# Modulation columns on VectorE alone, in another order, in a three-block transformer kernel

## The chip, the core and the metric

The kernel runs on one core of a Trainium2 chip. TensorE multiplies matrices into PSUM banks, VectorE and ScalarE work on SBUF and PSUM, GpSimd on SBUF; SyncE's queue issues the loads of weights, GpSimd's queue the gathers. The metric is the time of one execution in microseconds (us) as the device measures it; lower is better.

## The reference, cut to what matters

Two transformer blocks over 256 image tokens (x) and, in the first, 256 context tokens (ctx), then a third block of another kind. Width 1024, all float32.

```
def _modulation(cvec, w_mod, b_mod):
    m = jax.nn.silu(cvec) @ w_mod + b_mod
    return jnp.split(m[:, None, :], 6, axis=-1)
...
    for l in range(DEPTH):
        m_x = _modulation(c, w_mod[l], b_mod[l])
        m_c = _modulation(c_ctx[None, :], w_mod[l], b_mod[l])
        h = _modulate(x, norm1_g[l], m_x[0], m_x[1])
        hc = _modulate(ctx, norm1_g[l], m_c[0], m_c[1])
        if last:
            kv_c = _ctx_keys_values(hc, lp)
        else:
            mix_c, kv_c = _token_mix(hc, lp, None, None)
        mix_x, _ = _token_mix(h, lp, ang, kv_c)
        x = x + m_x[2] * mix_x
        h2 = _modulate(x, norm2_g[l], m_x[3], m_x[4])
        x = x + m_x[5] * _peer(h2, w_pq[l], peer_keys[l], peer_down[l], peer_up[l])
        if not last:
            ctx = ctx + m_c[2] * mix_c
            hc2 = _modulate(ctx, norm2_g[l], m_c[3], m_c[4])
            ctx = ctx + m_c[5] * _peer(hc2, ...)
```

A modulation has 6 x 1024 numbers: 48 columns of 128 (one column on 128 partitions), each the product of 128 rows of a weight matrix (512 KB) with silu(c). Columns 0 to 15 (shift and scale of the first norm) are `FIRST`; the rest are needed from the end of the mix on. `_token_mix` is latent attention, a Fourier and a pooling branch under gates, and `_peer` selects 128 of 16384 experts for each token, whose rows (8 KB) are gathered from memory. The third block has the same modulation and experts, with windowed attention and an RWKV scan for its mix.

## The kernel before

Tokens are kept transposed (features on partitions), in two tiles of 128 tokens where the experts work. The code records operations; a list scheduler then puts each engine's in an order by priority (the length of what depends on an operation, plus a lift given to its stage), by planned positions of stages (`ORDER`) and by how many buffers of a name may be in use (`QUOTA`); all instructions then come from one line, L694. An engine carries out its own list strictly in order, SyncE its loads likewise.

The stages in order of time, with the profile's times of before: block 1 image mix (x0, 0 to about 459 us: set-up, modulations, projections, gates, attention), expert selection and gathers for the image (p0, p0g) with the context's mix (c0) beside them, experts of the context (q0, q0g, to 1960), the rest of block 2's image mix (x1, y1), its experts (p1, p1g, 2119 to 2790), the third block's mix (b2, to 3338), its experts (p2, p2g). An expert stage is 256 gathers, 128 for each tile, of 1 MB each by GpSimd's queue; VectorE makes the dot products with `h2tok` (the tile's tokens as rows) and part of the weighted sum into `accd`.

`mods(wt, cols, outs)` (L795) makes columns: it loads the 512 KB of a column into a `wm` buffer, and for each output either VectorE multiplies and accumulates in one instruction (`scalar_tensor_tensor` with `accum_out`), or GpSimd multiplies into `mp` and ScalarE sums up; then one add of the bias on 128x1. `emit` (L1803) calls it so: `FIRST` of block 1 for the image on VectorE and the context on GpSimd, before both h; columns 16 to 47 likewise (m0); then, with a lift of -1000, block 2's `FIRST` for both, its columns 16 to 47 for the image, and the third block's `FIRST`, all on VectorE (m1: 32 + 32 + 16 columns); and after the second expert stage the third block's columns 16 to 47 on GpSimd (n2). `load_c` makes silu(c) on all partitions (`cb`). `kvproj` projects keys and values; `mix` makes the gates and the sums of gated branches `x0y` (eight pairs of instructions on VectorE), `mix_attend` attention and the output. `gather` (L1234) clears `accd` for both tiles, and makes a tile's `h2tok` (eight transposes on TensorE, two copies on ScalarE) when its turn comes.

Of the kernel before, what the change touches and what calls it, by code (L numbers as in the profile page):

```python
# [15 lines left out]
BF16 = mybir.dt.bfloat16  # L16
AF = mybir.ActivationFunctionType
OP = mybir.AluOpType
# [678 lines left out]
class Kern:  # L697
# [70 lines left out]
    def setup(self):  # L768
# [12 lines left out]
        self.junk = [self.t([P, D], f"junk{i}", 1, BF16) for i in range(2)]  # L781
# [13 lines left out]
    def mods(self, wt, cols, outs, bufs=6):  # L795

        for j in cols:
            w = self.w(wt[j], "wm", bufs)
            for m, cb, b, eng in outs:
                o = m[:, j:j + 1]  # L800
                if eng is self.nc.vector:
                    eng.scalar_tensor_tensor(self.junk[0], w, 1.0, cb, op0=OP.mult, op1=OP.mult, accum_out=o)
                else:
                    q = self.t([P, D], "mp", 2)
                    eng.tensor_tensor(q, w, cb, op=OP.mult)
                    self.nc.scalar.activation(self.junk[1], q, AF.Copy, accum_out=o)
                eng.tensor_tensor(o, o, b[:, j:j + 1], op=OP.add)
# [5 lines left out]
    def mods2(self, m2, cols, eng):  # L813
        self.mods(self.A["wada"], cols, [(m2, self.cb2, self.col("ada_b"), eng)])
# [419 lines left out]
    def gather(self, sel, n, tab, xT, g2, erf):  # L1234
# [3 lines left out]
        accs = [self.t([P, D], f"accd{i}", bufs=1) for i in range(-(-n // P))]  # L1238
        for i, acc in enumerate(accs):
            self.ahead(i)  # L1240
            nc.gpsimd.memset(acc, 0.0)
        for i in range(NT):
            m = min(P, n - i * P)
            if m <= 0:
                break
            self.ahead(i)
# [6 lines left out]
            acc = accs[i][:m]  # L1253
# [549 lines left out]
def emit(K, out, stage=None):  # L1803
# [9 lines left out]
    if stage in ("mix2", "b2"):  # L1813
        K.begin("x0", {}, "x0")
        K.load_cb2()
        K.mods2(m2, FIRST + list(range(16, 48)), nc.vector)
        return block2(K, out, stage, m2)
# [33 lines left out]
    both = [(modx[0], cbs[0], bm[0], nc.vector), (modc[0], cbs[1], bm[0], nc.gpsimd)]  # L1851
    K.mods(A["wmod0"], FIRST, both)
    K.load_mix(0)
    h = norm1(xT, modx[0], 0)
    hc = K.ln(cT, K.gscale(modc[0], 8, n1[0], "gsc"), modc[0][:, 0:8], name="c")
    K.kvproj(0, hc, 0, False)
    K.kvproj(0, h, T, True)
# [4 lines left out]
    K.begin("m1", {}, "m1", None, -1000)  # L1862
    K.mods(A["wmod1"], FIRST, [(modx[1], cbs[0], bm[1], nc.vector), (modc[1], cbs[1], bm[1], nc.vector)])
    K.mods(A["wmod1"], range(16, 48), [(modx[1], cbs[0], bm[1], nc.vector)])
    K.load_cb2()
    K.mods2(m2, FIRST, nc.vector)

# [34 lines left out]
    K.begin("n2", {}, "n2", "q0g")  # L1902
    K.load_cb2()
    K.mods2(m2, range(16, 48), nc.gpsimd)
# [15 lines left out]
def block2(K, out, stage, m2):  # L1920
    nc, A, xT = K.nc, K.A, K.xT
    K.begin("b2", {"ps": 6, "pt": 2}, "b2", "p1s")
    h = K.ln(xT, K.gscale(m2, 8, K.col("norm1_g_2"), "gsc"), m2[:, 0:8], spans=TILES)
# [180 lines left out]
```

## Time and profile before

| | us |
|---|---|
| median of 3 runs | 4013.39 (4008.55 to 4016.52) |
| profiled execution | 4016.26 |
| span of its profile | 4014.3 |
| TensorE busy | 2998.6 |
| VectorE busy | 2881.5 |
| ScalarE busy | 2077.3 |
| GpSimd busy | 1703.4 |

The mean granted clock of TensorE is 0.874 of full speed. 1305 MB are moved, 1074 MB of them by the gathers. In these pages PE is TensorE, PEld its weight loads, DVE VectorE, ACT ScalarE, POOL GpSimd, SP SyncE; "sb" is SBUF, "bank" a PSUM bank. An idle time stands in square brackets with what ended it. A row "x8" joins eight instructions one behind the other. A stretch is read for the engine that is busy nearly all of it, and where none is, for the rate of the DMA.

### The profile page before, as it was taken

How to read it: one execution, taken by the hardware profiler on the slowest of the kernel's cores; microseconds unless marked ns; L12 is line 12 of the kernel's file. 1: busy time of each engine (PE TensorE's matmuls, PEld its weight loads, DVE VectorE, ACT ScalarE, POOL GpSimd, SP SyncE). 2: the span in 40 equal slices, each digit the busy share in tenths (PEclk: the TensorE clock that was granted, in tenths of full speed). 3: DMA queues.
4: the chain of work that ended last, by engine and by line, in shares of the span. 5: the costliest groups of instructions: out<-in, count | busy, mean ns of one | idle time of the engine just before them, and what ended most of it. 6: DMA issues, size and time to landing. Idle time of an engine off the chain costs nothing. (4 is left out here: it accounts for less than half of the span.)

```text
span 4014.3 us, 40650 instructions
## 1 busy us (share of the span) xinstructions
PE 2998.6 (75%) x10928; PEld 1776.5 (44%) x10928; DVE 2881.5 (72%) x6733; ACT 2077.3 (52%) x6342; POOL 1703.4 (42%) x1325
## 2 busy tenths in 40 slices
PE   5769863597796589976698856666899998766755
PEld 4556731365473246632275422222677776322221
DVE  6697799977889985566547997666444438986566
ACT  4222455655655676566755667766544324433322
POOL 5470134545434444345553454554111113465454
PEclk7879875799998899998899988877899989888888
DMA  5557798999999999999757999999210017999998
GB/s 211 207 201 246 267 371 357 407 390 419 381 416 420 374 415 418 413 421 421 311 200 321 384 421 421 415 421 392 79 56 9 30 40 307 413 417 421 422 421 354
DMA packets 219828, 1305.42 MB, mean 325 GB/s; under 512 B 24336, under 2 KB 28880, under 8 KB 88272
## 3 DMA queue, kind: packets, MB, share of 16 engines
q0 software_dynamic: 147456, 1073.81, 64.9%
q1 hardware_dynamic: 72144, 229.02, 15.9%
q8 instruction: 89, 1.46, 0.1%
q14 instruction: 139, 1.14, 0.1%
HBM read 1301.68 MB, written 1.05 MB: 325 GB/s over the span
## 5 line engine op out<-in xcount | busy, mean ns | idle before, releaser
L694 PE MATMUL bank<-sb 128*128 128x128 f32 (+6 forms) x10928 | 2998.6, 431 | 1009.3 <-ACT sb L694 894.9
L694 PEld LDWEIGHTS bank<-sb 128*128 128x128 f32 (+4 forms) x10928 | 1776.5, 197 | 2231.0 <-ACT sb L694 1342.6
L694 DVE SCALAR_TENSOR_TENSOR sb<-sb 128x1024 f32<-128x1024 f32 (+4 forms) x1794 | 2052.0, 1171 | 670.7 <-DMA sb<-in_tab_dram,sb 538.0
L694 ACT ACTIVATE sb<-sb 128x1 f32<-128x1 f32 (+3 forms) x5415 | 1682.3, 319 | 1315.5 <-DVE sb L694 1053.3
L694 POOL DMA_INDIRECT sb<-in_tab_dram,sb x1024 | 1344.8, 1313 | 1582.2 <-PE bank L694 781.5
L694 POOL TENSOR_TENSOR sb<-sb 128x256 f32<-128x256 f32 (+2 forms) x288 | 350.7, 1248 | 546.2 <-DVE sb L694 213.9
L694 ACT ACTIVATE sb<-bank 128x256 f32<-128x256 f32 (+6 forms) x458 | 182.3, 414 | 359.6 <-PE bank L694 331.1
L694 DVE TENSOR_TENSOR sb<-sb 128x32 f32<-128x32 f32 (+13 forms) x1035 | 309.4, 332 | 18.8 <-ACT sb L694 12.6
L694 ACT ACTIVATE sb<-bank,sb 128x256 f32<-128x256 f32 (+3 forms) x223 | 104.0, 474 | 245.8 <-PE bank L694 141.3
L694 DVE SCALAR_TENSOR_TENSOR sb<-bank,sb 128x128 f32<-128x128 f32 (+3 forms) x186 | 64.9, 380 | 121.5 <-ACT sb L694 77.5
L694 DVE TENSOR_TENSOR sb<-bank,sb 128x64 f32<-128x64 f32 (+5 forms) x180 | 72.6, 422 | 101.5 <-PE bank L694 97.8
L694 ACT ACT_TABLE_LOAD x102 | 130.9, 1283 | 5.6 <-DVE sb L694 1.6
L694 DVE TENSOR_TENSOR sb<-sb,bank 128x512 f32<-128x512 f32 (+1 forms) x96 | 56.7, 597 | 79.4 <-PE bank L694 76.3
L694 DVE FIND_INDEX8 sb<-sb 128x8 uint32<-128x128 f32 (+1 forms) x384 | 96.7, 260 | 0.0
L694 DVE DVE_READ_ACCUMULATOR sb<-sb 128x1 f32 x1152 | 94.8, 82 | 0.0
L694 DVE MAX8 sb<-sb 128x8 f32<-128x128 f32 (+1 forms) x384 | 84.7, 255 | 11.6 <-ACT sb L694 10.8
L694 DVE TENSOR_SCALAR sb<-sb 128x128 f32<-128x128 f32 (+6 forms) x232 | 57.0, 256 | 41.1 <-DMA sb<-in_cols_dram 16.9
L694 DVE TENSOR_REDUCE sb<-sb 128x16 f32<-128x800 f32 (+3 forms) x120 | 74.7, 634 | 0.1
L694 POOL MEMSET sb<- 128x1024 f32 x8 | 7.6, 955 | 156.9 <-PE bank L694 126.7
L694 DVE SCALAR_TENSOR_TENSOR sb<-sb,bank 128x256 f32<-128x256 f32 (+1 forms) x88 | 30.8, 368 | 44.2 <-PE bank L694 39.1
L694 DVE MATCH_VALUE_LOAD sb<-sb 128x8 f32 x576 | 46.6, 81 | 0.2 <-DVE sb L694 0.2
L694 DVE MATCH_REPLACE8 sb<-sb 128x128 f32<-128x128 f32 (+1 forms) x192 | 46.5, 250 | 0.0
(14 smaller groups left out, 112.3 us busy)
## 6 DMA issues: line engine op xcount, KB each, us to landing
sb<-in_win_dram SPq DMA_DIRECT2D x116, 512.0 KB
sb<-in_wmod_dram SPq DMA_DIRECT2D x96, 512.0 KB
sb<-in_wpq_dram SPq DMA_DIRECT2D x64, 512.0 KB
sb<-in_wada_dram SPq DMA_DIRECT2D x48, 512.0 KB
sb<-in_wout_dram SPq DMA_DIRECT2D x32, 512.0 KB
sb<-in_tab_dram,sb POOLq DMA_INDIRECT x1024
sb<-in_wo_dram SPq DMA_DIRECT2D x48, 256.0 KB
sb<-in_poolm_dram SPq DMA_DIRECT2D x6, 512.0 KB
```

The costliest lines, as they stand in the source:

```text
L694: getattr(getattr(nc, op.eng), op.meth)(*[res(x) for x in op.args], **{k: res(x) for k, x in op.kw.items()})
```

## The change

All columns are made by VectorE, and the bias is added once for eight columns. The image's `FIRST` columns of block 1 stand by themselves, then the image's `kvproj`, then the context's `FIRST` (their matrices loaded a second time) and its h and `kvproj`. m0 makes image and context columns from one load. m1 keeps block 2's `FIRST` for both (32 columns), without its negative lift. Block 2's columns 16 to 47 of the image and the third block's `FIRST` (48 columns) become n1, which waits for the end of the second expert stage; silu(c) is loaded again for it. The third block's columns 16 to 47 become n2 within that block. `gather` clears `accd` and makes `h2tok` for both tiles ahead of the first gather. Some quotas and positions follow.

```diff
     def mods(self, wt, cols, outs, bufs=6):
+        vec, left = self.nc.vector, {}
+        for j in cols:
+            left[j // 8] = left.get(j // 8, 0) + 1
         for j in cols:
             w = self.w(wt[j], "wm", bufs)
-            for m, cb, b, eng in outs:
-                o = m[:, j:j + 1]
-                if eng is self.nc.vector:
-                    eng.scalar_tensor_tensor(self.junk[0], w, 1.0, cb, op0=OP.mult, op1=OP.mult, accum_out=o)
-                else:
-                    q = self.t([P, D], "mp", 2)
-                    eng.tensor_tensor(q, w, cb, op=OP.mult)
-                    self.nc.scalar.activation(self.junk[1], q, AF.Copy, accum_out=o)
-                eng.tensor_tensor(o, o, b[:, j:j + 1], op=OP.add)
+            left[j // 8] -= 1
+            for m, cb, b in outs:
+                vec.scalar_tensor_tensor(self.junk, w, 1.0, cb, op0=OP.mult, op1=OP.mult, accum_out=m[:, j:j + 1])
+            if not left[j // 8]:
+                c = slice(j // 8 * 8, j // 8 * 8 + 8)
+                for m, cb, b in outs:
+                    vec.tensor_tensor(m[:, c], m[:, c], b[:, c], op=OP.add)
...
     (gather)
-        accs = [self.t([P, D], f"accd{i}", bufs=1) for i in range(-(-n // P))]
-        for i, acc in enumerate(accs):
+        heads = []
+        for i in range(-(-n // P)):
+            m = min(P, n - i * P)
             self.ahead(i)
+            acc = self.t([P, D], f"accd{i}", bufs=1)[:m]
             nc.gpsimd.memset(acc, 0.0)
-        for i in range(NT):
-            m = min(P, n - i * P)
-            if m <= 0:
-                break
-            self.ahead(i)
             h2 = self.t([P, D], f"h2tok{i}", bufs=1)[:m]
...
-            acc = accs[i][:m]
+            heads.append((m, acc, h2))
+        for i, (m, acc, h2) in enumerate(heads):
+            self.ahead(i)
...
-    'm1wm': 3, 'n2wm': 3, ... 'b2L': 16, ... 'b2Tm': 6, ... 'b2p': 5,
+    'm1wm': 3, 'n1wm': 3, 'n2wm': 2, ... 'b2L': 4, ... 'b2Tm': 4, ... 'b2p': 4,
...
     (ORDER)
-    'n2': (1880, 2244),
-    'b2': (3516, 4152), 
+    'n1': (1880, 2244), 'n2': (3560, 3900), 'b2x': (3527, 4152),
+    'b2': (3516, 3527),
...
     (emit)
-    both = [(modx[0], cbs[0], bm[0], nc.vector), (modc[0], cbs[1], bm[0], nc.gpsimd)]
-    K.mods(A["wmod0"], FIRST, both)
+    both = [(modx[0], cbs[0], bm[0]), (modc[0], cbs[1], bm[0])]
+    K.mods(A["wmod0"], FIRST, both[:1])
     K.load_mix(0)
     h = norm1(xT, modx[0], 0)
+    K.kvproj(0, h, T, True)
+    K.mods(A["wmod0"], FIRST, both[1:])
     hc = K.ln(cT, K.gscale(modc[0], 8, n1[0], "gsc"), modc[0][:, 0:8], name="c")
     K.kvproj(0, hc, 0, False)
-    K.kvproj(0, h, T, True)
...
-    K.begin("m1", {}, "m1", None, -1000)
-    K.mods(A["wmod1"], FIRST, [(modx[1], cbs[0], bm[1], nc.vector), (modc[1], cbs[1], bm[1], nc.vector)])
-    K.mods(A["wmod1"], range(16, 48), [(modx[1], cbs[0], bm[1], nc.vector)])
-    K.load_cb2()
-    K.mods2(m2, FIRST, nc.vector)
+    K.begin("m1", {}, "m1")
+    K.mods(A["wmod1"], FIRST, [(modx[1], cbs[0], bm[1]), (modc[1], cbs[1], bm[1])])
...
-    K.begin("n2", {}, "n2", "q0g")
+    K.begin("n1", {}, "n1", "q0g")
+    cb = K.t([P, D], "cb0", 1)
+    K.load_c(cb, A["c"])
+    K.mods(A["wmod1"], range(16, 48), [(modx[1], cb, bm[1])])
     K.load_cb2()
-    K.mods2(m2, range(16, 48), nc.gpsimd)
+    K.mods2(m2, FIRST)
...
     (block2, behind its first norm)
+    if stage is None:
+        K.begin("n2", {}, "n2", None, -100)
+        K.load_cb2()
+        K.mods2(m2, range(16, 48))
+        K.begin("b2", {"ps": 6, "pt": 2}, "b2x")
```

How the lists of instructions change is shown at three places, as they stand in a row; "x5" is five of one kind.

VectorE at the start of the program, from the first column on, before (SCALAR_TENSOR_TENSOR 128x1024 is a column, 128x1 a bias add or a gain of a norm, 128x256 a part of h):

```order
L694 SCALAR_TENSOR_TENSOR sb_61<-sb_61 128x1024 x5
L694 TENSOR_TENSOR sb_61<-sb_61 128x1 x2
L694 SCALAR_TENSOR_TENSOR sb_61<-sb_61 128x1
L694 TENSOR_TENSOR sb_61<-sb_61 128x1
L694 SCALAR_TENSOR_TENSOR sb_61<-sb_61 128x256
L694 SCALAR_TENSOR_TENSOR sb_61<-sb_61 128x1
L694 TENSOR_TENSOR sb_61<-sb_61 128x1
L694 SCALAR_TENSOR_TENSOR sb_61<-sb_61 128x256
```

and after, from the same place:

```order
L694 SCALAR_TENSOR_TENSOR sb_61<-sb_61 128x1024 x5
L694 TENSOR_TENSOR sb_61<-sb_61 128x1024
L694 TENSOR_SCALAR sb_61<-sb_61 128x14
L694 TENSOR_SCALAR sb_61<-sb_61 128x4
L694 TENSOR_SCALAR sb_61<-sb_61 128x1
L694 TENSOR_SCALAR sb_61<-sb_61 128x4
L694 SCALAR_TENSOR_TENSOR sb_61<-sb_61 128x1024 x11
L694 TENSOR_TENSOR sb_61<-sb_61 128x8 x2
L694 SCALAR_TENSOR_TENSOR sb_61<-sb_61 128x1 x2
L694 SCALAR_TENSOR_TENSOR sb_61<-sb_61 128x256 x2
```

Before, columns, bias adds and parts of h alternate. After, five columns and then eleven stand in a row with a few small operations on constants between, behind them two adds of eight columns, and then gains and parts of the image's h; the context's columns come after the h.

GpSimd at the start, before (128x1024 are the products of the context's columns, 128x256 sums of gated branches):

```order
L694 TENSOR_TENSOR sb_61<-sb_61 128x1024 x15
L694 TENSOR_TENSOR sb_61<-sb_61 128x1
L694 TENSOR_TENSOR sb_61<-sb_61 128x1024
L694 TENSOR_TENSOR sb_61<-sb_61 128x1 x15
L694 TENSOR_TENSOR sb_61<-sb_61 128x1024 x7
L694 TENSOR_TENSOR sb_61<-sb_61 128x256
```

and after, to the gathers of the first expert stage (DMA from the expert table):

```order
L694 IOTA sb_61 128x128
L694 TENSOR_TENSOR sb_61<-sb_61 128x256 x8
L694 MEMSET sb_61 128x1024 x2
L694 DMA sb_61<-in_tab0_dram,sb_61 128x2048 x125
L694 TENSOR_TENSOR sb_61<-sb_61 128x256
```

No product and no bias add is left on GpSimd; behind the eight sums follow the two clearings and the first gathers.

SyncE's loads in the third block, before (win2 and wva2 are its weights, abias the attention's bias, wpq2 the weights of its expert selection):

```order
L694 DMA sb_61<-in_win2_dram 128x1024 x2
L694 DMA sb_61<-in_wva2_dram 128x1024 x4
L694 DMA sb_61<-in_win2_dram 128x1024 x17
L694 DMA sb_61<-in_abias_dram 128x512 x2
L694 DMA sb_61<-in_win2_dram 128x1024 x3
L694 DMA sb_61<-in_abias_dram 128x512 x5
L694 DMA sb_61<-in_wpq2_dram 128x1024
```

and after (wada is the third block's modulation matrix, one load for each column):

```order
L694 DMA sb_61<-in_win2_dram 128x1024 x4
L694 DMA sb_61<-in_wada_dram 128x1024 x2
L694 DMA sb_61<-in_win2_dram 128x1024 x2
L694 DMA sb_61<-in_wada_dram 128x1024 x3
L694 DMA sb_61<-in_win2_dram 128x1024
L694 DMA sb_61<-in_wada_dram 128x1024
L694 DMA sb_61<-in_win2_dram 128x1024
L694 DMA sb_61<-in_wada_dram 128x1024 x4
L694 DMA sb_61<-in_win2_dram 128x1024 x2
L694 DMA sb_61<-in_wada_dram 128x1024
L694 DMA sb_61<-in_win2_dram 128x1024
```

Loads of columns now stand between the block's own weights, one to four at a time.

## Rows read from the trace of the kernel before

**Rows 1.** table by stretch: engines busy us (instructions), clock, DMA share, GB/s

```profile
20.00:97.00 77.00, 38.40 (x142) 29.75 (x141) 61.34 (x75) 30.33 (x53) 50.86 (x32) 0.76 0.50 172
97.00:142.00 45.00, 44.65 (x188) 32.34 (x187) 6.05 (x14) 16.90 (x36) 0.00 (x0) 1.00 0.43 142
142.00:311.00 169.00, 104.57 (x380) 80.84 (x379) 165.37 (x231) 48.18 (x91) 126.85 (x73) 0.80 0.65 229
311.00:460.00 149.00, 137.01 (x914) 110.04 (x915) 103.81 (x350) 45.55 (x113) 2.08 (x3) 0.97 0.62 213
460.00:1960.00 1500.00, 1101.39 (x3346) 635.04 (x3344) 1198.59 (x2781) 930.84 (x3076) 680.16 (x529) 0.87 0.99 402
1961.00:2120.00 159.00, 134.75 (x802) 96.75 (x802) 76.56 (x223) 96.17 (x221) 84.00 (x68) 0.95 0.52 179
2811.00:3338.00 527.00, 498.79 (x3046) 382.40 (x3047) 220.75 (x603) 207.28 (x472) 78.99 (x106) 0.92 0.13 44
```

**Rows 2.** timeline of GpSimd: gathers at stage ends (start, us, operation)

```profile
459.37 1.13 POOL L694 DMA_INDIRECT sb<-in_tab_dram,sb  x1 [47.51 <-DVE sb L694]
...
1960.33 0.94 POOL L694 DMA_INDIRECT sb<-in_tab_dram,sb  x1 [0.41 <-PE bank L694]
...
2119.32 0.99 POOL L694 DMA_INDIRECT sb<-in_tab_dram,sb  x1 [12.80 <-DVE sb L694]
```

**Rows 3.** VectorE groups, 0 to 350 us: busy us, mean ns, idle before

```profile
L694 DVE SCALAR_TENSOR_TENSOR sb<-sb 128x1024 bf16<-128x1024 f32 x99 | 188.7, 1906 | 11.7 <-DMA sb<-in_wmod_dram 9.9
L694 DVE TENSOR_TENSOR sb<-sb 128x1 f32<-128x1 f32 x89 | 38.1, 469 | 0.2
```

**Rows 4.** GpSimd's products, 0 to 350 us

```profile
L694 POOL TENSOR_TENSOR sb<-sb 128x1024 f32<-128x1024 f32 x48 | 147.0, 3086 | 89.6 <-DMA sb<-in_wmod_dram 59.4 <-DMA sb<-in_win_dram 19.9 <-ACT sb L694 10.2
```

**Rows 5.** timeline of VectorE, the first columns (start, us, operation)

```profile
20.86 1.22 DVE L694 SCALAR_TENSOR_TENSOR sb<-sb 128x1024 bf16<-128x1024 f32 x1
...
22.12 3.24 DVE L694 SCALAR_TENSOR_TENSOR sb<-sb 128x1024 bf16<-128x1024 f32 x1
```

**Rows 6.** timeline of GpSimd, its first three products

```profile
21.02 9.81 POOL L694 TENSOR_TENSOR sb<-sb 128x1024 f32<-128x1024 f32 x3 [19.94 <-DMA sb<-in_win_dram]
```

**Rows 7.** timeline of VectorE: image gains, context h and keys, columns, last sum

```profile
79.80 2.12 DVE L694 SCALAR_TENSOR_TENSOR sb<-sb 128x1 f32<-128x1 f32 x8
...
116.66 1.35 DVE L694 SCALAR_TENSOR_TENSOR sb<-sb 128x256 f32<-128x256 f32 x3 [12.67 <-PE bank L694]
...
136.11 0.48 DVE L694 SCALAR_TENSOR_TENSOR sb<-bank,sb 128x256 f32<-128x256 f32 x1 [12.92 <-ACT sb L694]
...
141.51 1.23 DVE L694 SCALAR_TENSOR_TENSOR sb<-sb 128x1024 bf16<-128x1024 f32 x1 [4.91 <-DMA sb<-in_wmod_dram]
...
142.77 1.23 DVE L694 SCALAR_TENSOR_TENSOR sb<-sb 128x1024 bf16<-128x1024 f32 x1
...
310.28 0.42 DVE L694 SCALAR_TENSOR_TENSOR sb<-sb,bank 128x256 f32<-128x256 f32 x1
```

**Rows 8.** timeline of TensorE, its first matmuls on the image's h

```profile
80.47 3.73 PE L694 MATMUL bank<-sb 128*128 128x256 f32 x8 [5.71 <-ACT sb L694]
```

**Rows 9.** VectorE's columns, 310 to 460 us

```profile
L694 DVE SCALAR_TENSOR_TENSOR sb<-sb 128x1024 bf16<-128x1024 f32 x39 | 47.6, 1220 | 19.4 <-DMA sb<-in_wmod_dram 17.1 <-DMA sb<-in_wada_dram 2.0
```

**Rows 10.** first stage at its change of tile: GpSimd gather, table by stretch

```profile
873.16 0.94 POOL L694 DMA_INDIRECT sb<-in_tab_dram,sb  x1 [11.08 <-DVE sb L694]
...
880.00:890.00 10.00, 8.87 (x22) 4.95 (x23) 8.27 (x13) 8.02 (x28) 2.63 (x2) 0.69 0.99 392
890.00:900.00 10.00, 10.00 (x44) 8.06 (x43) 7.20 (x10) 6.23 (x22) 5.09 (x4) 1.00 0.87 300
```

**Rows 11.** timeline of VectorE in the pause after the second stage

```profile
1988.62 7.45 DVE L694 SCALAR_TENSOR_TENSOR sb<-sb 128x256 f32<-128x256 f32 x8 [6.79 <-ACT sb L694]
...
2006.27 6.78 DVE L694 COPY sb<-sb 32x512 f32<-32x512 f32 x8 [0.95 <-ACT sb L694]
```

**Rows 12.** waits of VectorE, 2811 to 3338 us

```profile
DVE sb L694 <- PE bank L694: 196.1, 143, 9.8
```

More of the change, by code (lines that the diff above doesn't have):

```diff
@@ L780, in setup @@
             nc.vector.memset(self.eps[:, i:i + 1], v)
-        self.junk = [self.t([P, D], f"junk{i}", 1, BF16) for i in range(2)]
+        self.junk = self.t([P, D], "junk", 1, BF16)
         self.iota = self.t([P, P], "iota", 1)
@@ L811, in load_cb2, with mods2 @@
         self.load_c(self.cb2, self.A["c_2"])
-    def mods2(self, m2, cols, eng):
-        self.mods(self.A["wada"], cols, [(m2, self.cb2, self.col("ada_b"), eng)])
+    def mods2(self, m2, cols):
+        self.mods(self.A["wada"], cols, [(m2, self.cb2, self.col("ada_b"))])
     def gscale(self, m, j, g, name):
@@ L1815, in emit @@
         K.load_cb2()
-        K.mods2(m2, FIRST + list(range(16, 48)), nc.vector)
+        K.mods2(m2, FIRST + list(range(16, 48)))
         return block2(K, out, stage, m2)
```

12 rows, old and new, of tables (FIFO, QUOTA) are left out of this document.

## The prediction

> **What bounds the kernel now.** I read the table by stretches first, since the page's shares average over stages with different limits. [rows 1] shows the stages: from 142 to 311 us VectorE is busy 165.4 of 169 us, TensorE 104.6 and DMA moves 229 GB/s, so VectorE is the bound there; from 311 to 460 TensorE is (137.0 of 149); from 460 to 1960 the gathers of the first two expert stages move 402 GB/s and neither TensorE (1101 of 1500) nor VectorE (1199) is full; from 1961 to 2120 and from 2811 to 3338 TensorE leads again (134.8 of 159; 498.8 of 527) with VectorE half idle (76.6; 220.8) and DMA at 179 and 44 GB/s. A gain of VectorE at the start therefore counts in full up to the first gather at 459.4 us [rows 2]; after that the gathers follow one another as before and the gain is carried along.
>
> Next, what fills VectorE at the start. 99 multiply-accumulates of a modulation column (SCALAR_TENSOR_TENSOR, 128x1024) take 188.7 us, 1906 ns each, and 89 adds of one bias 38.1 us [rows 3]. Beside them GpSimd runs 48 products of the same size at 3086 ns [rows 4]. The time of one instruction has two values: 1.22 us at 20.86, before GpSimd's first product begins at 21.02, and 3.24 us at 22.12 beside it [rows 5, 6]; at 141.51 and 142.77, with GpSimd idle, 1.23 us and a next start 1.26 us later [rows 7]. So a column on VectorE costs 1.26 us of the engine alone, and the GpSimd half of the work is paid for by the VectorE half: 99 x (1.906 - 1.22) = 68 us lost, plus the slow adds.
>
> **The start: image h.** Before, the image's 16 first columns run from 20.86 us beside the context's 16 on GpSimd; the gains of h come at 79.80 [rows 7]. After, 5 + 11 multiply-accumulates stand almost in one run in VectorE's list, and GpSimd has no product left. 20.86 + 16 x 1.26 = 41; to it come waits for their loads (VectorE waited 11.7 us ahead of these instructions before 350 us [rows 3]; I take 9) and the gains: about 52, 28 us earlier. The context's 16 columns now stand behind, 16 x 1.26 = 20 us on VectorE, while TensorE projects the image's h (66 matmuls; eight took 3.73 us [rows 8], so 31 us): context h at about 52 + 20 + 4 = 76. Before it stood at 116.66, and the normalised context keys followed at 136.11, 19.5 us later [rows 7]; I keep that distance and get 96, and take 97 for the moment from which the remaining columns run alone, against 141.51. The pessimistic end keeps the whole distance 79.80 to 141.51: 52 + 61.7 = 114. The context's matrices are loaded a second time, 16 x 0.52 = 8.4 MB; at 229 GB/s that is 37 us of transfer, beside 142 us of this stretch with room: nothing, as long as loads keep ahead.
>
> **The gate sums.** Between there and the last pair of gate sums VectorE's list holds 96 columns (64 of block 1, 32 of block 2), 8 pairs, some adds by eights: 96 x 1.26 + 8 x 0.75 + 2 = 129 us, so the last pair ends at 97 + 129 = 226. Before it ended at 310.28 + 0.42 = 310.7 [rows 7]. The term is **-84.7 us**. Bounds: 114 instead of 97 gives -68; loads without any wait at the start give -94. TensorE must do its part in the same time: 44.7 us of 97 to 142 and 104.6 of 142 to 311 [rows 1], 149 us together from about 52, so 201 at the earliest, below 226.
>
> **The attention behind it.** From 310 us on, 39 more columns (47.6 us [rows 9]) stand among attention's VectorE work; after, none. TensorE is busy 137.0 of 149 us there, so at most 12 us can go. I take **-7** (0 to -12). First gather: 459.4 - 84.7 - 7 = 368.
>
> **The heads.** The second tile's rows were made when its turn came: GpSimd's gather at 873.16 waited 11.08 us, and the DMA rate fell to 392 and 300 GB/s at 880 to 900, against 420 around it [rows 10]. (420-392)/420 x 10 + (420-300)/420 x 10 = 3.5 us of transfer time missing in one stage; its 1 MB gathers set the end. I take **-4** for all four stages (0 to -6).
>
> **The pause before the second block's expert stage.** From the last gather at 1960.33 to the first of the next at 2119.32 [rows 2] GpSimd made 32 columns; now VectorE makes 48: 48 x 1.26 = 60.5 us on an engine that had 159 - 76.6 = 82 us free. Against it stands what GpSimd inflated: the eight context products of 128x256 took 7.45 us and eight copies 6.78 [rows 11], where three of the former took 1.35 at 116.66 [rows 7], 0.45 each, so 3.6: about 4 us back on the chain. TensorE bounds the stretch, but each step of it that waits for VectorE may now find a 1.26 us column ahead of it in VectorE's queue; a dozen such steps at half a column are 8 us. And SyncE's queue holds this stage's query weights behind column loads that wait for a free buffer. I take **+3** (-8 to +20).
>
> **The pause in the third block.** 32 columns among work where VectorE waited 196.1 us for TensorE in 143 pieces [rows 12]. The columns fit into that, 32 x 1.26 = 40 us; some of them will stand ahead of a step that TensorE waits for, a dozen at half a column again 8 us. Behind each column's load (two buffers) wait the block's own weights on SyncE. I take **+6** (0 to +25). Smaller quotas of this block's buffers are inside that range.
>
> **Sum.** -84.7 - 7 - 4 + 3 + 6 = -86.7. The profiled run took 4016.3 us, so 3929.6; the median of the runs shown lies 2.9 us lower: **3927**. Ends of the terms together: 4013 - 68 + 20 + 25 = 3990 and 4013 - 94 - 12 - 6 - 8 = 3893; all bad at once is unlikely.
>
> **Rivals.** (A) VectorE is the full engine and is given more. Row 1906 ns stands for the instruction whoever works beside it: then 16 + 16 + 96 columns at 1.98 us are 253 us, the last pair ends at 20.9 + 253 + 9 + 8 = 291, and only about 20 + 7 us are gained: 3986. The 1.23 us at 141.51 speak against it. The Trainium skill, "Perfetto Trace Analysis", section "Optimizing Scalar/DVE Operations", says to offload from a saturated VectorE to ScalarE or even GpSimd, which is the contrary of this change; it adds that the two share a read port to SBUF, so that moving work between them might not help. By its first half the time would be that of A; rows 5 and 6 bear out the second half, 3.24 against 1.22 us. 0.05.
>
> (B) VectorE no longer waits for itself, but for loads. From 20 to 311 us 172 x 77 + 142 x 45 + 229 x 169 = 58 MB came in [rows 1]; with the 8.4 MB loaded again 67 MB must arrive by the last pair. At 402 GB/s, the rate of the gathers, that is done at 20 + 166 = 186 us, before VectorE; at 229 GB/s only at 20 + 291 = 311, and nothing is gained at the start. Half way between 226 and 311 the last pair ends at 268, and the time is 3927 + 42 = 3969. For it speaks that VectorE's waits at the start were mostly for modulation matrices [rows 3]; against it, that each matrix of the 96 columns' stretch serves two columns (context and image), so 48 loads in 129 us, 195 GB/s. 0.14.
>
> (C) Slower: the third block's chain. If each of the 32 columns stops a step of TensorE for a full column with its load (1.26 + 512 KB at the 229 GB/s of [rows 1], 2.3 us, together 3.5) because columns, weights and SyncE's queue wait for one another in order, the block grows by 32 x 3.5 = 113 us: 3921 + 113 = 4034. It decides once the block's 527 us grow by more than 92. Against it: VectorE idle for over half of the block and DMA at 44 GB/s. 0.03.
>
> (D) The pause at 1961 takes its 60 us in series: 3927 - 3 + 60 = 3984. It would need TensorE to wait for most columns. 0.06.
>
> **How the numbers follow.** The forecast has 0.72 with 3893 to 3960; B reaches to 3969. The range 3893 to 3970 holds the forecast's 0.72 and most of B, over 0.8. 0.2% (8 us) is about what a measurement of this kernel can tell from no change. Faster: 0.72 + 0.05 + 0.14 + 0.06 less a little for mixtures of C and D = 0.94; slower 0.04; same 0.02.
>
> **What would show it.** The mean of a 128x1024 multiply-accumulate before 350 us near 1.22 us; image gains near 52, last pair near 226, first gather near 368; the pause from last to first gather near 160; the third block near 533. It is wrong if VectorE's waits for modulation matrices grow at the start (B), or if the means stay near 1.9 (A).

## The result and the profile after

The changed kernel takes 3948.1 us (median of 4 runs, 3942.1 to 3953.2) against 4013.7; the ratio is 0.9838, with a 95% interval of 0.9818 to 0.9857. That is 65.6 us less, where 86.7 were forecast. The profiled run took 3951.7 us with a span of 3949.7. One execution in all that follows (noheads_order) took 12350 us; no ratio and no profile here uses it.

Five stretches of the changed kernel, with the columns of [rows 1]: from the remaining columns to the last gate sums, attention, the first two expert stages, the pause behind them, the third block.

```profile
97.00:234.00 137.00, 122.70 (x514) 97.12 (x513) 126.44 (x223) 18.42 (x39) 9.33 (x8) 0.95 0.80 287
234.00:373.00 139.00, 132.19 (x894) 107.12 (x894) 57.65 (x227) 43.84 (x112) 2.21 (x3) 0.97 0.18 61
373.00:1890.00 1517.00, 1100.36 (x3361) 636.60 (x3360) 1198.56 (x2780) 932.30 (x3079) 691.23 (x529) 0.88 0.98 397
1890.00:2054.00 164.00, 140.79 (x830) 102.33 (x830) 116.20 (x331) 67.83 (x160) 2.35 (x2) 0.93 0.66 233
2720.00:3274.00 554.00, 502.73 (x3066) 380.57 (x3066) 271.41 (x689) 214.81 (x507) 89.52 (x108) 0.92 0.24 79
```

VectorE is now free for 10 us of the 137 of the first of them, and TensorE is close behind it (122.7); in the second TensorE is as full as in [rows 1] (132.2 of 139), with VectorE down from 103.8 to 57.7 us. In the pause and in the third block VectorE carries what was put there: 116.2 us of the pause instead of 76.6, and 270.9 instead of 233.7 of the third block from last to first gather (rows in n2_in_pause below).

The columns on VectorE up to 350 us, as in [rows 3]:

```profile
L694 DVE SCALAR_TENSOR_TENSOR sb<-sb 128x1024 bf16<-128x1024 f32 x128 | 158.3, 1237 | 26.5 <-DMA sb<-in_wmod_dram 22.8
```

128 columns at 1237 ns stand where 99 took 1906. The milestones that answer to [rows 7], on VectorE's timeline: the image's gains and h, the context's keys, the first of the 96 remaining columns, the last gate sum:

```profile
49.04 5.16 DVE L694 SCALAR_TENSOR_TENSOR sb<-sb 128x1 f32<-128x1 f32 x17
...
93.00 0.48 DVE L694 SCALAR_TENSOR_TENSOR sb<-bank,sb 128x256 f32<-128x256 f32 x1 [8.65 <-ACT sb L694]
...
97.12 1.23 DVE L694 SCALAR_TENSOR_TENSOR sb<-sb 128x1024 bf16<-128x1024 f32 x1 [3.64 <-DMA sb<-in_wmod_dram]
...
232.85 0.42 DVE L694 SCALAR_TENSOR_TENSOR sb<-sb,bank 128x256 f32<-128x256 f32 x1 [0.79 <-ACT sb L694]
```

And the gathers of [rows 2]: the first of the first stage, the last of the second, the first of the next:

```profile
373.07 1.09 POOL L694 DMA_INDIRECT sb<-in_tab_dram,sb  x1 [45.23 <-DVE sb L694]
...
1890.48 1.40 POOL L694 DMA_INDIRECT sb<-in_tab_dram,sb  x1 [1.09 <-PE bank L694]
...
2054.12 0.95 POOL L694 DMA_INDIRECT sb<-in_tab_dram,sb  x1 [7.98 <-ACT sb L694]
```

Read by the starts of the first and last gathers, and by the span, the 64.6 us between the two profiled spans come together like this (us):

| | before | after | difference | forecast |
|---|---|---|---|---|
| start to the last gate sum | 310.7 | 233.3 | -77.4 | -84.7 |
| attention, to the first gather | 148.7 | 139.8 | -8.9 | -7 |
| first two expert stages | 1501.0 | 1517.4 | +16.4 | -4 (of all four) |
| pause | 159.0 | 163.6 | +4.6 | +3 |
| expert stage of block 2 | 671.0 | 666.4 | -4.6 | 0 |
| third block, to its first gather | 548.0 | 553.4 | +5.4 | +6 |
| its expert stage and the end | 675.9 | 675.8 | -0.1 | 0 |

A second profile of each of the two kernels shows how far a stage moves between executions of one program: the first two expert stages took 1501.6 us in the kernel before and 1506.7 in the changed one, the pause 162.6 and 164.9, the third block 540.8 and 560.0; the first gather came at 457.9 and 372.5. So the start is firm to 1.5 us, the two expert stages only to 11, the pause to 4 and the third block to 7.

### The profile page after: what moved, and what is told of

It is laid out like the page before. It is cut to its first block, busy times and chain, and to the rows that moved or that the text cites. A ratio compares the mean times of both kernels' runs of the same rounds, so it can differ in the third digit from the quotient of the medians.

```text
span 3949.7 us, 40304 instructions
## 1 busy us (share of the span) xinstructions
PE 2966.0 (75%) x10928; PEld 1760.1 (45%) x10928; DVE 2858.3 (72%) x6792; ACT 1992.4 (50%) x6181; POOL 1485.3 (38%) x1165
## 4 chain that ended last, share of the span: by engine, by line
DVE 24%; issue 20%; POOL 15%; PE 15%; DMA 14%; ACT 4%; POOLq 0%; DVEq 0%; SPq 0%; ACTq 0%
DVE sb L694 24%; POOL sb L694 15%; PE bank L694 15%; DMA sb<-in_tab_dram,sb 11%; ACT sb L694 2%; ACT L694 1%; DMA sb<-in_wada_dram 1%; DMA sb<-in_wmod_dram 1%; DMA sb<-in_wo_dram 1%; POOLq L694 0%; DMA sb<-in_win_dram 0%; DMA sb<-in_wpq_dram 0%; DVEq L694 0%; SPq L694 0%; DVEq L2104 0%
## 5 line engine op out<-in xcount | busy, mean ns | idle before, releaser
L694 PE MATMUL bank<-sb 128*128 128x256 f32 (+8 forms) x10928 | 2966.0, 428 | 977.4 <-ACT sb L694 907.7
L694 PEld LDWEIGHTS bank<-sb 128*128 128x128 f32 (+5 forms) x10928 | 1760.1, 196 | 2182.9 <-ACT sb L694 1353.3
L694 DVE SCALAR_TENSOR_TENSOR sb<-sb 128x1024 f32<-128x1024 f32 (+4 forms) x1874 | 2073.0, 1133 | 708.4 <-DMA sb<-in_tab_dram,sb 551.2
L694 ACT ACTIVATE sb<-sb 128x1 f32<-128x1 f32 (+3 forms) x5336 | 1603.9, 308 | 1289.4 <-DVE sb L694 1109.8
L694 POOL DMA_INDIRECT sb<-in_tab_dram,sb x1024 | 1363.6, 1332 | 1569.0 <-PE bank L694 808.7
L694 ACT ACTIVATE sb<-bank 128x256 f32<-128x256 f32 (+5 forms) x458 | 182.9, 414 | 351.3 <-PE bank L694 315.3
L694 POOL TENSOR_TENSOR sb<-sb 128x256 f32<-128x256 f32 x128 | 113.5, 909 | 596.7 <-DVE sb L694 426.7
L694 DVE TENSOR_TENSOR sb<-sb 128x32 f32<-128x32 f32 (+12 forms) x934 | 273.6, 322 | 8.0 <-ACT sb L694 4.5
L694 DVE TENSOR_TENSOR sb<-bank,sb 128x512 f32<-128x512 f32 (+5 forms) x180 | 72.1, 421 | 84.7 <-PE bank L694 74.5
L694 DVE TENSOR_SCALAR sb<-sb 128x1 f32<-128x1 f32 (+7 forms) x232 | 50.0, 225 | 41.1 <-PE bank L694 17.3
```

The source lines that it names most:

```text
L694: getattr(getattr(nc, op.eng), op.meth)(*[res(x) for x in op.args], **{k: res(x) for k, x in op.kw.items()})
```

## The experiments

### Each kernel once more

The two kernels unaltered, for a second profile; the stages are in the paragraph above.

> The changed kernel once more, unaltered, for a second profile: how far does a stage move between two executions of one program? The first profile had 1517 us from the first gather of the first expert stage to the last of the second, against 1501 before. Plan theory (the 16 us belong to the changed lists): 1513 to 1521 again. Noise theory (executions of one program differ by that much in the gathers): anything from 1500 to 1530.

> The kernel before once more, unaltered, for a second profile. Plan theory: 1497 to 1505 us for the first two expert stages, first gather at 459. Noise theory: anything from 1490 to 1520.

3950.0 and 4010.8 us. For the kernel before the stages came as the plan theory said (1501.6). For the changed one they took 1506.7 us, outside the 1513 to 1521 of the plan theory and inside the noise theory's range: 11 of the 16 us are no more than two executions of one program differ by, and 5 are left.

### The other kernels

Three questions: does the start gain by leaving GpSimd alone, or by order; why did the first two expert stages, whose work is the same, grow; and what do the columns cost where they now stand. The table gives for each kernel the same stretches (us), each row from one profiled execution; medians and intervals stand with the experiments.

| kernel | first gather | first two expert stages | pause | block 2's experts | third block |
|---|---|---|---|---|---|
| before | 459.4 | 1501.0 | 159.0 | 671.0 | 548.0 |
| after | 373.1 | 1517.4 | 163.6 | 666.4 | 553.4 |
| ctx_gpsimd | 439.4 | 1518.7 | 164.0 | 664.9 | 559.3 |
| first_together | 373.2 | 1512.9 | 160.6 | 664.4 | 550.7 |
| rows7 | 366.6 | 1519.9 | 158.8 | 668.1 | 558.2 |
| after_noheads | 369.5 | 1580.9 | 161.7 | 662.6 | 551.0 |
| noheads_order | 366.4 | 1576.9 | 158.8 | 663.9 | 559.7 |
| after_order | 376.2 | 1521.5 | 163.4 | 664.0 | 560.1 |
| before_heads | 474.6 | 1527.8 | 158.5 | 657.9 | 524.5 |
| before_rows6 | 474.0 | 1514.4 | 165.1 | 671.2 | 524.3 |
| n1_at_start | 395.3 | 1501.0 | 146.8 | 668.3 | 558.7 |
| n2_in_pause | 373.9 | 1509.7 | 160.0 | 768.8 | 520.8 |

### The context's columns on GpSimd again

```diff
             for m, cb, b in outs:
+                if m is self.pool:
+                    q = self.t([P, D], "mp", 2)
+                    self.nc.gpsimd.tensor_tensor(q, w, cb, op=OP.mult)
+                    self.nc.scalar.activation(self.junk1, q, AF.Copy, accum_out=m[:, j:j + 1])
+                    continue
                 vec.scalar_tensor_tensor(...)
...
+    K.pool = modc[0]
```

> The changed kernel with the context's 48 columns of block 1 made by GpSimd and ScalarE again, in the changed kernel's order of the code. Contention theory: the columns on VectorE beside a product take over 3 us again, their mean at the start rises from 1.24 to near 1.9 us, and the first gather comes some 20 to 40 us later than the 373 of the changed kernel. Rival (VectorE is simply the full engine): with 48 columns less, 60 us of its work, it comes earlier, at 330 to 360.

One run, 4023.9 us. VectorE's columns and GpSimd's products up to 330 us, and the first gather:

```profile
L694 DVE SCALAR_TENSOR_TENSOR sb<-sb 128x1024 bf16<-128x1024 f32 x80 | 156.8, 1960 | 15.5 <-DMA sb<-in_wmod_dram 13.1
...
L694 POOL TENSOR_TENSOR sb<-sb 128x1024 f32<-128x1024 f32 x48 | 140.9, 2966 | 92.9 <-DVE sb L694 48.7 <-DMA sb<-in_wmod_dram 36.1 <-ACT sb L694 8.0
```

Two of VectorE's columns, without and with a product beside them:

```profile
117.75 1.23 DVE L694 SCALAR_TENSOR_TENSOR sb<-sb 128x1024 bf16<-128x1024 f32 x1 [5.49 <-DMA sb<-in_wmod_dram]
...
122.82 3.25 DVE L694 SCALAR_TENSOR_TENSOR sb<-sb 128x1024 bf16<-128x1024 f32 x1
```

```profile
439.36 1.12 POOL L694 DMA_INDIRECT sb<-in_tab_dram,sb  x1 [62.65 <-DVE sb L694]
```

VectorE has 80 columns instead of 128 and still is busy with them for as long (156.8 against 158.3 us), at 1960 ns each. The 43 columns that overlap no product take 1.22 us in the mean, the 37 that overlap one 2.82. The first gather comes 66 us later, more than the 20 to 40 that were expected: the 48 products take 141 us of GpSimd's time, and the context's h needs the first sixteen, so the remaining columns start at 117.75 instead of 97.1. So of the 86 us of the start some 66 come from taking GpSimd out, with the order of the code left as it is in the changed kernel; they hold both GpSimd's slower products and VectorE's longer columns, which this run does not part. The other 20 are about what the 48 columns cost that left the start (22 us in n1_at_start below). The Trainium skill, "SBUF — State Buffer", section "Who interferes with whom", has a VectorE instruction with two inputs from SBUF contend with a GpSimd instruction that reads SBUF; this trace agrees, 1.96 against 1.24 us.

### The image's first 16 columns by themselves, or not

```diff
-    K.mods(A["wmod0"], FIRST, both[:1])
+    K.mods(A["wmod0"], FIRST, both)
...
-    K.mods(A["wmod0"], FIRST, both[1:])
```

> The changed kernel with the first 16 columns of image and context made together from one load again, ahead of both h, all on VectorE. If the image's own head start counts: the image's h is ready 16 x 1.26 = 20 us later, near 73 instead of 53, TensorE starts that much later, and the first gather comes up to 20 us later than 373, at 385 to 393. If VectorE's total is what counts, and the second load of 8.4 MB is what the split costs: the first gather stays at 373 or comes up to 5 us earlier.

One run, 3939.5 us. The first gather stands at 373.2 against 373.1: the head start of the image's h and the second load of 8.4 MB came to nothing together. VectorE's total was the bound; the image's h came 7 us later (60.4 instead of 53.1), the context's 13.5 us earlier (70.9 instead of 84.4), and the 96 columns began at 91.0 instead of 97.1. That the whole run lies 2.6 us under the fastest of the changed kernel is one execution and settles nothing.

### Seven gather buffers in the first expert stage

The number of buffers of a name is the larger of its quota and of what is alive at once in the recorded order. With the heads that gave 6 gather buffers (1 MB each) in the first expert stage, without them 7. Two kernels test whether the lost buffer is where the 16 us went, from both sides:

```diff
 (rows7, on the changed kernel, in QUOTA)
+    'p0rows': 7,
 (before_rows6, on the kernel before, where the buffers are counted)
             tg.n = min(max(tg.quota, int(tg.occ.max())), len(tg.tiles))
+            if tg.name == 'p0rows':
+                tg.n = 6
```

> The changed kernel with one number more: the quota of the first expert stage's gather buffers (p0rows) is 7. Without it the changed kernel has 6 and the kernel before had 7, because the count is the larger of the quota and of what is alive at once in the recorded order, and that order changed with the heads. Buffer theory: the sixth of the 1 MB buffers is not enough to cover a delayed VectorE; from first gather to the next stage's first the 801.7 us of the changed kernel come back to the 784.4 of before, and the median falls from 3948 by some 17 us to about 3931. List theory: the loss comes from a new order of the context's attention between the gathers, whatever the buffers; the stage stays near 800 us and the median at 3948.

> The kernel before with 6 gather buffers in the first expert stage instead of 7, and nothing else. Buffer theory: 784 us grow to about 800, median about 4030. List theory: 4014 within 4 us.

rows7: 3949.3 us, ratio 0.9838 (0.9811 to 0.9864), the same as the changed kernel. Its first tile of the first stage did become faster (370.9 us from first to first gather, against 390.3 and 382.9 in the two profiles of the changed kernel), but the next stage's first tile gave it back (387.4 against 368.3 and 367.7); the two stages together stay at 1519.9. before_rows6: 4034.2 us, ratio 1.0069 (1.0044 to 1.0093), slower by about what was expected. Its profile is of an execution of 4025.4 us, the shortest of nine: the two stages were 13 us longer, but the first gather also came 15 us later, in a stretch that uses no gather buffer, and the third block was 24 us shorter. So the edit gave other lists everywhere and is no test of the buffer alone. By the stretch that the expectations named, from the first gather to the next stage's first, both runs went as the buffer theory said: 788.1 us with seven buffers (801.7 and 791.1 in the changed kernel's two profiles), 798.2 with six (784.4 and 784.8 in those of before). Against it, n1_at_start has six and takes 782.2. The buffer may cost some of the first stage; that it explains the sum of the two stages is not shown, since rows7 did not get it back.

### The heads alone, and the change without them

> The changed kernel with the gather function of before: a tile's token rows are made when its turn comes, and the first expert stage has 7 gather buffers by that. Buffer theory: the stage takes about 784 us, plus or minus the 3.5 us that the change of tile cost: 3931 to 3935. List theory: the loss stays, and the heads' 4 us are lost in addition: about 3952.

> The kernel before with the heads alone (both tiles' rows made ahead of the first gather); it then has 6 gather buffers in the first expert stage instead of 7. Buffer theory: slower by the 17 us that the changed kernel lost there, less the 3.5 us of the change of tile: about 4027. List theory: the heads only save their 4 us: about 4010.

The edit is the `gather` of the other kernel. after_noheads: 4005.3 us, ratio 0.9979 (0.9961 to 0.9996), so 57 us slower than the changed kernel, against 4 that were forecast for the heads. The table by stretch, 750 to 900 us, of after_noheads, and behind it 800 to 900 of the changed kernel:

```profile
750.00:800.00 50.00, 43.80 (x189) 34.07 (x187) 14.54 (x27) 12.46 (x37) 11.86 (x11) 1.00 0.79 304
800.00:850.00 50.00, 47.27 (x216) 40.22 (x214) 3.37 (x8) 5.68 (x12) 2.89 (x4) 1.00 0.41 134
850.00:900.00 50.00, 41.34 (x187) 29.77 (x187) 28.32 (x79) 26.71 (x98) 5.42 (x6) 0.97 0.39 137
```

```profile
800.00:850.00 50.00, 39.40 (x135) 27.01 (x134) 32.34 (x44) 25.05 (x84) 23.65 (x19) 0.90 1.00 402
850.00:900.00 50.00, 40.20 (x150) 28.63 (x149) 35.58 (x49) 29.66 (x99) 23.82 (x19) 0.97 1.01 414
```

From 800 to 850 us 134 GB/s move instead of 402, with TensorE nearly full. These are no gathers but loads of weights: GpSimd issues no gather from 767 to 880.7 us. What stands on TensorE then, two rows of its timeline; what VectorE waited for between 780 and 880 us; the second tile's rows on ScalarE, and GpSimd's last gather before and first behind this hole of 114 us:

```profile
783.79 13.29 PE L694 MATMUL bank<-sb 128*128 128x256 f32 x60 [1.77 <-DMA sb<-in_win_dram]
...
826.98 23.12 PE L694 MATMUL bank<-sb 128*128 128x256 f32 x106 [0.33 <-DMA sb<-in_win_dram]
```

```profile
DVE sb L694 <- ACT sb L694: 81.2, 14, 13.2
```

```profile
871.75 0.60 ACT L694 ACTIVATE sb<-bank 128x512 f32<-128x512 f32 x1 [0.76 <-PE bank L694]
```

```profile
765.89 0.95 POOL L694 DMA_INDIRECT sb<-in_tab_dram,sb  x1 [0.17 <-issue]
...
880.72 1.69 POOL L694 DMA_INDIRECT sb<-in_tab_dram,sb  x1 [18.75 <-DVE sb L694]
```

From 784 us on TensorE works through the context's projections, 128x256 matmuls by the dozen; the transposes of the second tile stand behind and among them in its list, the copies into the second tile's rows come at 872, and only then do dot products set gather buffers free. VectorE waits meanwhile on ScalarE for the context's gates. In the kernel before the same copies came at 862, but in the middle of the context's work, with 11 us of waiting in front of the gather of [rows 10]. So the wait of before was no measure of what the heads are worth behind the new start.

before_heads: 4035.9 us, ratio 1.0064 (1.0034 to 1.0093): slower, by more than either theory said. Its ten executions spread from 4018.2 to 4057.9 us, and the profile is of one of 4019.8: first gather 15 us later, the two stages 27 us longer, block 2's experts 13 and the third block 24 us shorter. The heads alone don't help the kernel before; where the slower executions lose their time is not shown.

### The same work planned by the ranks of the kernel before

If a new plan of unchanged work is the cause, the old plan should heal it. Two kernels give the planner, for every instruction from the first to the end of the second expert stage, the rank that it had in the plan before as its priority:

```diff
+        for op, (name, key) in zip(self.rec, _keys(self, self.rec)):
+            if name in FIRST_SEGS:
+                op.prio += 1e12
+            elif key in rank:
+                op.prio = 1e11 - 4000.0 * rank[key]
```

> The same instructions as the changed kernel without heads (after_noheads, 4005 us, 1581 us from the first gather of the first expert stage to the last of the second, against 1501 in the kernel before with the same code there). Only the planner's priorities differ: from the first expert stage to the second's end it takes the ranks that the plan of the kernel before gave to the same instructions, so that the engines' lists there come near to those of before. List theory (a stage whose code is unchanged gets other lists when the start changes, and these cost tens of us): the two stages come back to about 1505 us and the median to about 3930. Rival (the shorter start leaves something undone, loads or h, that the stages must then make up): they stay above 1560 and the median near 4000.

> The changed kernel with heads, its lists from the first expert stage to the second's end planned by the ranks of the kernel before, heads left early; 6 gather buffers as in the changed kernel. List theory: 1517 us for the two stages become about 1500, the median about 3931. Rival (6 buffers or the heads themselves cost the 16 us): they stay at 1515 to 1520 and the median at 3948.

noheads_order: 3994.3 us, ratio 0.9952 (0.9935 to 0.9968); the two stages take 1576.9 us, not 1505. Its table by stretch has the same low rates:

```profile
737.00:800.00 63.00, 59.55 (x251) 43.24 (x250) 15.45 (x28) 15.56 (x47) 11.68 (x11) 1.00 0.67 253
800.00:850.00 50.00, 47.03 (x212) 39.24 (x211) 2.95 (x7) 5.21 (x11) 2.18 (x3) 1.00 0.45 144
850.00:900.00 50.00, 36.29 (x138) 24.58 (x137) 28.96 (x46) 26.13 (x90) 16.45 (x14) 0.94 0.60 229
```

after_order: 3948.4 us, ratio 0.9837 (0.9808 to 0.9867); 1521.5 us for the two stages, in a profiled execution of 3963.2. Neither came back. As priorities the ranks bring the lists nearer to those of before (by the planner's lists from the first expert stage to the second's end, VectorE's instructions stand on average 13 places from there instead of 46 in noheads_order, 4 instead of 13 in after_order), but they don't repeat them, and TensorE's list still holds the context's projections ahead of the transposes. The exact old order was not tried, so the theory is neither shown nor ruled out; lists nearer to the old ones did not bring the old time back.

### The columns of the first pause back at the start

```diff
+    K.begin("m1", {}, "m1", None, -1000)
+    K.mods(A["wmod1"], range(16, 48), [(modx[1], cbs[0], bm[1])])
+    K.load_cb2()
+    K.mods2(m2, FIRST)
...
-    K.begin("n1", {}, "n1", "q0g")
 ...
```

> The changed kernel with the 48 columns of the first pause back at the start, behind everything there as in the kernel before (lift -1000), still all on VectorE. If they are off the path there, since VectorE was busy 14 to 19 of 50 us between 250 and 350: first gather at 373 to 383, and the pause from 163.6 us to about 158. If keeping them out of the start is part of the gain: the first gather up to 48 x 1.26 = 60 us later, 400 to 433.

One run, 3948.6 us, the same. From the last gate sums to the first gather, and the pause:

```profile
234.00:395.00 161.00, 137.21 (x897) 111.12 (x897) 111.53 (x330) 46.96 (x116) 3.02 (x4) 0.94 0.65 219
1896.00:2043.00 147.00, 130.08 (x802) 95.91 (x802) 60.33 (x219) 62.71 (x155) 2.82 (x4) 0.98 0.26 92
```

The first gather came at 395.3, between the two ranges that were expected, and the pause fell to 146.8, further than the 158. The 48 columns cost 22 us at the start (161 us where the changed kernel has 139) and 17 in the pause (163.6 against 146.8); neither place hides them, and the move is worth nothing or little. The two expert stages took 1501.0 us here, as in the kernel before. TensorE is busy 137 of 161 and 130 of 147 us: it had room only for part of them.

### The columns of the third block in the pause

```diff
-    K.mods2(m2, FIRST)
+    K.mods2(m2, FIRST + list(range(16, 48)))
...
-        K.begin("n2", {}, "n2", None, -100)
-        K.load_cb2()
-        K.mods2(m2, range(16, 48))
```

> The changed kernel with the third block's 32 columns moved out of that block into the pause after the second expert stage, which then has 80. If columns cost where they stand: the third block, 553 us from the last gather ahead of it to the first behind it, falls to about 547, and the pause grows from 164 us by 11 (the 48 columns there cost 17 against the kernel that has them at the start, 0.35 each) to about 175. If the block hides them: 553 stays and the kernel is 11 us slower, near 3959.

One run, 4009.6 us, 50 us above the higher of the two expectations. The pause did not grow (160.0), but the next expert stage did, by 102 us. GpSimd's timeline there:

```profile
2054.69 0.96 POOL L694 DMA_INDIRECT sb<-in_tab_dram,sb  x1 [0.30 <-issue]
...
2184.19 0.95 POOL L694 MEMSET sb<- 128x1024 f32 x1 [128.54 <-DVE sb L694]
```

After eight gathers it waits 128.5 us for VectorE, which had 33 columns still to make after 2044 us, among the tiles' selection; the ninth gather comes at 2196. The pause has no room for 80 columns, and what does not fit holds up the gathers (418 GB/s move once they run, from 2196 to 2812 us). The third block without the columns took 520.8 us, 33 less than in the changed kernel, where 6 were expected. Rows of the third block from last to first gather, of before, before_rows6, n2_in_pause and the changed kernel:

```profile
2790.30:3338.30 548.00, 509.89 (x3064) 385.91 (x3065) 233.71 (x621) 219.48 (x511) 80.38 (x107) 0.91 0.15 52
```

```profile
2824.70:3349.00 524.30, 486.60 (x3048) 368.59 (x3049) 233.29 (x621) 215.72 (x501) 80.34 (x108) 0.95 0.17 56
```

```profile
2812.80:3333.50 520.70, 481.22 (x3054) 366.82 (x3055) 235.00 (x632) 215.07 (x502) 81.09 (x108) 0.95 0.17 54
```

```profile
2720.50:3273.90 553.40, 502.40 (x3064) 380.47 (x3065) 270.88 (x687) 214.37 (x506) 89.43 (x107) 0.92 0.24 79
```

before and before_rows6 have the same work there, in lists that are the same but for a few instructions, and differ by 24 us: the granted clock is 0.91 in the one and 0.95 in the other, and TensorE is busy 509.9 or 486.6 us for it. The low clock of before lies elsewhere than that of the changed kernel. 400 to 450 us into the block it is 0.69 and 0.67 in the two profiles of before, 0.93 in before_rows6, and 1.00 in the changed kernel and in n2_in_pause. 140 to 300 us into the block, behind most of the columns (they stand at 75 to 180), it is the other way round. Here are this stretch of before and of the changed kernel, and a row of TensorE's timeline in the latter:

```profile
2930.30:3090.30 160.00, 153.38 (x941) 115.11 (x941) 70.23 (x171) 63.33 (x139) 29.73 (x41) 0.98 0.09 30
```

```profile
2860.50:3020.50 160.00, 143.46 (x785) 106.24 (x783) 72.49 (x178) 55.55 (x124) 20.28 (x27) 0.82 0.20 63
```

```profile
2867.45 17.32 PE L694 MATMUL bank<-sb 128*128 128x256 f32 x64 [6.50 <-DMA sb<-in_win_dram]
```

TensorE waits 6.5 us for one of the block's own weights, whose loads SyncE issues between those of the columns; towards the end of this wait the clock falls, and it is 0.82 in the mean of the stretch. All nine profiles with columns in the block have such a wait (4.2 to 6.8 us) and a clock of 0.75 to 0.87 in this stretch; the five without have at most 1.4 us and 0.96 to 0.99. So 32 columns cost the block 33 us by n2_in_pause (39 by the changed kernel's second profile), not the 5 us by which the two kernels differ. That the wait for the weight brings the low clock is likely but not shown by itself. VectorE's waits there:

```profile
DVE sb L694 <- PE bank L694: 170.5, 133, 9.8
...
DVE sb L694 <- DMA sb<-in_wada_dram: 14.0, 16, 1.7
```

It waits 170.5 us for TensorE where it waited 196.1 [rows 12], so some 26 of the 41 us of columns went into those waits; 14.0 us it waits for their loads.

## Why the forecast was right, and where it was not

**The bound and the price of a column.** Right. VectorE was the bound, and 1.26 us a column held (1237 ns, and 1.27 from start to start). Rival A, that the instruction costs what it costs, falls: its mean is 1237 ns, and ctx_gpsimd brings the 1960 back. The Trainium skill, "Perfetto Trace Analysis", section "Optimizing Scalar/DVE Operations", says of moving work of a full VectorE to GpSimd only that it may make sense, with the warning about the shared port; here the warning held, and the move would cost 66 us.

**Image h, context h, the 96 columns.** Image gains at 49 to 54 (52 said), context h at 84 (76), the context's keys at 93.0 (96), first of the 96 columns at 97.1 (97). The last sum came at 233.3, not 226. VectorE's waits from 97 to 234 us:

```profile
DVE sb L694 <- DMA sb<-in_wmod_dram: 9.2, 7, 3.6
```

3.6 of these 9.2 us lie ahead of the first of the 96 columns, so waits for modulation matrices make 5.6 of the missing 7. Ahead of the columns up to 350 us they grew from 9.9 us [rows 3] to 22.8, which the prediction had named as the sign of B: "loads keep ahead" did not quite hold, and rival B came in small, at 5.6 of its 42 us. The reason I gave for the early start, the image's own 16 columns, was not needed: first_together reaches the same 373 without it.

**Attention.** -8.9 for -7, inside 0 to -12: TensorE is full.

**The step that failed: "the gathers follow one another as before and the gain is carried along", and the -4 of the heads.** The first two expert stages were 16.4 us longer (5.1 between the second profiles), not shorter. Of the 22 us by which the gain fell short in the profiles, this makes 20 and the start 7; attention and block 2's experts gave some back. I took an unchanged stage as a constant and sized the heads by the one wait that the trace of before shows. Both are wrong: the planner makes new lists for the whole program, the 602 MB, the 1100 us of TensorE and the 1199 of VectorE stayed, and still the twelve kernels with this work take from 1501 to 1581 us for it. The heads are worth 57 us behind the new start and cost 22 in the kernel before. Why the changed kernel's stages are 5 to 16 us longer than before stays open. A seventh buffer (rows7) and the old ranks (after_order) did not bring the sum back, n1_at_start took 1501.0 with the heads and six buffers, and the changed kernel's own two profiles differ by 10.7.

**The pauses.** +4.6 for +3, and +5.4 for +6. The first size was near for the reason given: n1_at_start shows the price of the 48 columns as 17 of their 60 us, and the earlier GpSimd work there had cost almost as much (159.0 against 146.8). The second was near by luck. Without the 32 columns the changed kernel's block takes 33 us less (n2_in_pause), so the step that they fit into VectorE's waits, but for 8 us, was too cheap by far. What stands behind it is what the prediction named for its upper end, the block's weights behind the columns' loads, with a lower clock behind. It did not show, because the block of before was itself 24 us longer than that of before_rows6, mostly at a low clock of its own (0.69 and 0.67, 400 to 450 us in), which the changed kernel does not have. Rivals C (113 us) and D (60 us) did not come in full.

## What to carry to other kernels

Before work goes to a second engine to relieve a full one, read the duration of the same instruction with and without the neighbour: here 99 instructions of VectorE took half as long again in the mean with 48 products on GpSimd beside them, and doing all of it on the full engine was the faster way. A short wait in a trace says what a thing cost in that order of the lists, not what it protects from: price it again behind whatever the change puts in front. And where a planner rewrites the lists, "the rest moves along" needs a margin of its own: 1% of these stages here, 5% in the worst build, which several builds of the same work show better than one profile. A term that comes out right is checked by taking its cause away: the third block's 5 us were 33 for the columns less what the clock gave back elsewhere.

## What was not expected of the hardware

With nearly the same lists, the third block, bound by TensorE, takes 548.0 us at a mean granted clock of 0.91 and 524.3 at 0.95 (rows above). These are means over stretches at its two levels, 1.2 and 2.4 GHz. Most of the difference lies 400 to 450 us into the block: 0.69 in before, 0.67 in its second profile, 0.93 in before_rows6 and in before_heads. TensorE was busy 98.2 of the 100 us ahead of it in before, and 98.7 in before_rows6, so the busy time alone does not tell the two apart. Why the clock falls there in one build and not in the other stays open.
